# Four places of a one-core hybrid decoder layer re-ordered: a broadcast behind the first scores, two accumulating transfers ahead of a split, one weight copy behind a sum's copy, and the last eighteen row groups summed row by row

## The chip, the cores and the metric

The kernel runs on one core of one Trainium2 chip. The metric is the device time of one execution in microseconds (us). The kernel before was run three times for this; the median is 1169.59 us (1168.78 to 1170.29). One more execution was profiled, and every start, duration and wait below is from that one.

The engines are named as the profile names them: PE is TensorE's matrix multiplication, PEld its weight load, DVE is VectorE, ACT is ScalarE, POOL is GpSimd and SP is SyncE. A letter q behind an engine's name means its instruction queue, such as where it issues a DMA. L1112 is line 1112 of the kernel before.

## The reference, cut to what matters

One layer over 1024 positions of width 1024, all in float32:

```python
h = rmsnorm(x, mix_norm)
q, k, v, su, sv, g_a, g_b = jnp.split(h @ w_in, splits, axis=-1)
y_att = sliding_window_attention(q, k, v, q_norm, k_norm, sinks)     # 8 heads, 2 kv heads, window 128
y_sgu = chunked_spatial_gating(su, sv, sgu_norm, w_s, b_s)
merged = sigmoid(g_a) * (y_att @ w_oa) + sigmoid(g_b) * (y_sgu @ w_ob)
x = x + merged @ w_out
z = rmsnorm(x, ffn_norm) @ w_up                                      # 1024 -> 2 * 2816
zc = conv_b + sum(conv_w[tap] * shifted(z, tap) for tap in range(3)) # causal, by channel
gate, val = jnp.split(zc, 2, axis=-1)
x = x + (silu(gate) * val) @ w_down                                  # 2816 -> 1024
```

## The kernel before

**Precision.** Every float32 operand is kept as two float32r tiles, a high part (an ACT copy, helper `copy_hi`, L88) and a low part (operand minus high part, mostly a subtraction on POOL or DVE). A product is three matmuls: high by high, high by low, low by high.

**Fast products.** The large dense products are cut into 2 by 2 blocks and done with seven block products in place of eight (Strassen's scheme in Winograd's form). The blocks of the left operand are called A11, A12, A22 and the sums S1 to S4, those of the right one B11, B21, B22 and T1 to T4. One block product of the MLP's first half is twelve matmuls of 128x512 (`Blocks.prod`, L1112): four slices of the contraction by three.

**Stages, in order of time.** Key and value projection with the queries (`q_proj`); sixteen attention steps with pieces of other projections between them as filler work for PE; the spatial gating; eight gate pairs; the two branch products; the output projection; the MLP's first half as 22 pairs (`first_pair` for pair 0, `fast_pair` for pairs 1 to 21), one pair being 256 columns of w_up, one gate chunk and one value chunk; and last the product with w_down, in 42 groups of two or one contraction chunks (`mms(g)`, seven block products of six groups each).

**What sets the order.** The order within each engine is that of the Python code, since all stages run under a manual schedule. Each engine takes its instructions one after another; one that waits holds up all behind it on that engine. PE, DVE, ACT, POOL and SP wait for each other by semaphores.

**Around the first place.** `rms_rows` (L135) spreads a column of reciprocal norms over 128 partitions: four small matmuls into a PSUM tile `rb`, then an ACT copy into `rstd_b`. It is called twice at the end of the projection stage, once for each half of the positions; behind it comes attention step 0, which begins with the score matmuls `sc` (`s_mm(0)`) and goes on with a query projection `pq`. The second `rb` takes over the PSUM slot of a transposed query tile that DVE is still splitting (`qs`, L345).

**Around the second place.** Per pair, the left operands come as `lp` (A11, A12) and `lq` (its two halves become S1 and A22) and `s3`. They are loaded by SP; two DMAs that POOL issues (`adds`, L1029 and L1030) then add further blocks of w_up onto `s3` and onto the first half of `lq`. POOL computes S2 and S4 (`sums_r`, into `lr`) and the low parts: `pl` of `lp`, `ql` of `lq` (`split_q`), `s3l`, and the low part of `lr` into the tile `AX` (`split_r`). In `first_pair`, POOL makes the sums of pair 1, then `ql` of pair 1, and then issues the adds for pair 2.

**Around the third place.** At the end of each pair, PE makes the product S2 into `v1`; DVE adds to it, ACT copies the sum into `u2` (L1124), DVE makes two differences and scales (L1130), ACT applies the convolution's last tap (`tap_v`, L1733) and after it copies the next pair's first product into `x1` (L1878). The next pair's A12 is accumulated onto the PSUM tile that this last copy reads. In the code before, the ACT copy of the weight split into `AX` (`split_r` of the next pair) stands ahead of the copy into `u2`.

**Around the last place.** The last block product, M3, adds into four PSUM row blocks X[0] to X[3], two to a PSUM tile (`pdx`). Each group goes through the four row blocks in turn; after the last group, DVE adds the residual into `res` for row blocks 0, 1, 2 (`plus`, L2064), each followed by its store, and then for row block 3 in two halves (L2087), the first stored by ACT and the second by SP.

Of the kernel before, what the change touches and what calls it, by code (L numbers as in the profile page):

```python
# [11 lines left out]
R = mybir.dt.float32r  # L12
# [28 lines left out]
def body(ctx, tc, nc, a):  # L41
# [37 lines left out]
    def PH(s):  # L79
        if psum.get("H") is None:  # L80
            return PS(s)[:, 0:512]
        return psum["H"].tile([128, 512], F, tag="H", name=nm(s))
# [379 lines left out]
    k_lo(1)  # L462
    rms_rows([PH("rb")], rstd, (1,))
    v_split()
# [225 lines left out]
    for n in range(20):  # L690
        if n < 16:
            s_mm(n)
            s_mask(n)
        if 0 <= n - 1 < 16:
            s_exp(n - 1)
# [307 lines left out]
    class Left:  # L1003
# [75 lines left out]
        def split_q(self):  # L1079
            self.split(("S1", "A22"), self.q, *(wst.tile([128, 8, 128], R, tag="w" + x, name=nm("q" + x))  # L1080
                                                for x in "hl"))

        def split_s3(self):
# [712 lines left out]
    def first_pair():  # L1796
# [44 lines left out]
        nx.split_s3()  # L1841
        nx.sums_r()
        nx.split_q()
        lefts[2].adds()
        lefts[2].load_p()
        nc.scalar.copy(u2, q.v1)
# [13 lines left out]
    def fast_pair(n, prev, q, hooks, rms=None):  # L1860
# [56 lines left out]
        if nx:  # L1917
            nx.split_q()
            nx.split_r(n + 1)
            if n + 3 < NPAIR:  # L1920
                lefts[n + 3].load_ahead()
        else:
            hooks[0]()
        q.prod(q.v1, "S2", "T2")
        q.sums(x1, x7, q.v0)
        if not nx:
            hooks[1]()
# [9 lines left out]
    def mlp():  # L1937
# [93 lines left out]
        def mms(g):  # L2031
# [8 lines left out]
            for k in range(k0, k1):  # L2040
                for d in range(4):
                    m = slice(128 * d, 128 * d + 128)
                    for j, (p, q) in enumerate(((ah, bh), (ah, bl), (al, bh))):
                        nc.tensor.matmul(o[d], p[:, k - k0, m], q[:, k - k0, :],  # L2044
                                         start=new and k == 0 and j == 0, stop=k == HK - 1 and j == 2,
                                         skip_group_check=True)

        rs = {}

# [18 lines left out]
        def done(s):  # L2068
            for d in range(4):
# [10 lines left out]
                if s == "M5":  # L2080
                    plus("C22", d, X[d], True)
                if s == "M3" and d < 3:
                    plus("C12", d, X[d], True)
                if s == "M3" and d == 3:
                    t = rs["C12"][:, d, :]
                    for q, c in ((nc.scalar, slice(0, 256)), (nc.sync, slice(256, 512))):
                        nc.vector.scalar_tensor_tensor(t[:, c], X[d][:, c], 0.5, t[:, c], op0=ALU.mult, op1=ALU.add)  # L2087
                        q.dma_start(a["out"][d, :, 512 + c.start:512 + c.stop], t[:, c])
            if s == "M1":
# [30 lines left out]
        for g in range(len(groups)):  # L2120
            mms(g)
            s, k0, k1 = groups[g]
# [25 lines left out]
            if g == 0:  # L2148
                q.tanh()

    with tc.manual_schedule():
# [80 lines left out]
```

## Time and profile before

| what | us |
|---|---|
| median of the three runs | 1169.59 |
| the profiled execution | 1169.8 |
| its span, from the first to the last instruction of the trace | 1168.0 |
| PE busy in the span | 1156.0 |
| POOL busy in the span | 661.0 |
| DVE busy in the span | 853.7 |
| ACT busy in the span | 589.7 |

The profiled execution's time has 1.8 us around the span. Rows of the timeline give the start and the duration of an instruction, its engine, line, operation, output and inputs, and in brackets how long the engine was idle before it and who ended that. Rows of the chain of waits give start, duration, engine, tile and line of the pieces that led to the end, each released by the one above it. A window row gives, for a stretch, each engine's busy time with the number of instructions, then the mean granted clock of TensorE (1.00 is full), the busy share of the DMA engines and their GB/s.

### The profile page before, as it was taken

What the parts mean: (1) busy time and instruction counts of PE and PEld (TensorE: products, weight loads), DVE (VectorE), ACT (ScalarE), POOL (GpSimd) and SP (SyncE); (2) the same over time, 40 slices, a digit from 0 to 9 for tenths busy, and PEclk for the clock granted to TensorE, in tenths of its full rate; (3) what the DMA queues carried; (4) which work ended last, traced back from release to release, by engine and by line L of the source; (5) the groups of instructions that cost most, each with busy time, mean ns of one, the idle gap of its engine ahead of it and who ended that gap; (6) DMA issues with size and microseconds to landing.
All of it is one profiled execution on the core that took longest, in us unless ns stands there. A gap on an engine that the chain in (4) does not pass through costs nothing.

```text
span 1168.0 us, 15816 instructions
## 1 busy us (share of the span) xinstructions
PE 1156.0 (99%) x5784; PEld 981.8 (84%) x5784; DVE 853.7 (73%) x985; ACT 589.7 (50%) x895; POOL 661.0 (57%) x461
## 2 busy tenths in 40 slices
PE   9999999999999999999899999999999999999998
PEld 9899999988888888888788888888888888888886
DVE  7777746734537889877778878887879787866674
ACT  6665568643436546686444444444444454425231
POOL 1668675598783854798776767767677640000000
PEclk9999999999999999999899999999999999999999
DMA  9442575256646766644554545554454368966561
GB/s 367 144 145 56 134 219 189 91 187 192 199 108 236 244 206 234 190 144 132 139 171 126 171 113 159 140 158 127 144 160 138 98 217 299 357 217 200 171 224 55
DMA packets 86429, 204.37 MB, mean 175 GB/s; under 512 B 9616, under 2 KB 17296, under 8 KB 86160
## 3 DMA queue, kind: packets, MB, share of 16 engines
q1 hardware_dynamic: 77280, 174.93, 43.3%
q0 software_dynamic: 8544, 19.93, 10.4%
q10 hardware_dynamic: 528, 8.52, 2.2%
q8 instruction: 45, 0.74, 0.3%
q14 instruction: 32, 0.26, 0.1%
HBM read 162.70 MB, written 57.41 MB: 188 GB/s over the span
## 4 chain that ended last, share of the span: by engine, by line
PE 90%; DVE 3%; POOL 3%; ACT 1%; DMA 1%; issue 1%; SPq 0%; DVEq 0%; POOLq 0%; ACTq 0%
PE pz L1112 51%; PE pdx L2044 10%; PE pd L2044 8%; PE pY L1692 2%; PE pX L1692 2%; PE pvs L94 1%; PE pvs L93 1%; PE pvs L92 1%; PE pu L94 1%; PE pu L92 1%; PE pu L93 1%; PE pv L560 1%; PE pq L92 1%; PE pq L94 1%; PE pq L93 1%
## 5 line engine op out<-in xcount | busy, mean ns | idle before, releaser
L1112 PE MATMUL pz<-T,qh 128*128 128x512 f32 x464 | 143.3, 390 | 0.0
L1112 PE MATMUL pz<-B,ph 128*128 128x512 f32 x352 | 110.5, 396 | 3.3 <-ACT x L1878 3.3
L1112 PEld LDWEIGHTS pz<-T,qh 128*128 128x128 f32 x464 | 87.3, 188 | 18.5 <-ACT u L936 0.3
L1071 POOL TENSOR_TENSOR pl<-lp,ph 128x1024 fp32r<-128x1024 f32 x30 | 72.6, 2421 | 42.5 <-ACT ph L88 42.5
L1112 PE MATMUL pz<-T,ql 128*128 128x512 f32 x232 | 90.3, 389 | 0.0
L1112 PEld LDWEIGHTS pz<-B,ph 128*128 128x128 f32 x352 | 66.9, 191 | 17.6 <-ACT x L1878 3.7
L1130 DVE TENSOR_TENSOR pz<-pz,rstd_b 128x1024 f32<-128x1024 f32 x60 | 74.0, 1233 | 6.1 <-ACT rstd_b L143 4.1
L1071 POOL TENSOR_TENSOR ql<-lq,qh 128x1024 fp32r<-128x1024 f32 (+1 forms) x30 | 75.7, 2522 | 0.1
L1112 PE MATMUL pz<-T,s3h 128*128 128x512 f32 x232 | 71.4, 389 | 0.0
L1112 PE MATMUL pz<-y,wjh 128*128 128x512 f32 x224 | 69.5, 391 | 0.3 <-POOL y L1286 0.3
L1112 PE MATMUL pz<-B,pl 128*128 128x512 f32 x176 | 69.5, 395 | 0.0
L2044 PE MATMUL pdx<-bh,ah 128*128 128x512 f32 x176 | 68.6, 390 | 0.1
L2044 PE MATMUL pdx<-bl,ah 128*128 128x512 f32 x176 | 68.5, 389 | 0.0
L2044 PE MATMUL pdx<-bh,al 128*128 128x512 f32 x176 | 68.5, 389 | 0.0
L88 ACT ACTIVATE qh<-lq 128x1024 fp32r<-128x1024 f32 (+1 forms) x30 | 31.4, 1047 | 69.6 <-POOL pl L1071 28.1
L1071 POOL TENSOR_TENSOR s3l<-lq,s3h 128x512 fp32r<-128x512 f32 x20 | 26.0, 1299 | 70.3 <-ACT s3h L88 70.3
L1352 POOL TENSOR_TENSOR wjl<-wj,wjh 128x512 fp32r<-128x512 f32 (+1 forms) x32 | 42.0, 1334 | 33.6 <-ACT wjh L88 26.9
L1112 PE MATMUL pz<-T,AX 128*128 128x512 f32 x252 | 60.5, 389 | 0.0
L1112 PE MATMUL pz<-B,AX 128*128 128x512 f32 x252 | 60.5, 389 | 0.0
L1738 DVE SCALAR_TENSOR_TENSOR tv<-pz,cp,tv 128x1023 f32<-128x1023 f32 (+1 forms) x44 | 56.2, 1278 | 0.8
L1738 DVE SCALAR_TENSOR_TENSOR tg<-pz,cp,tg 128x1023 f32<-128x1023 f32 (+1 forms) x44 | 56.2, 1278 | 0.8
L1112 PEld LDWEIGHTS pz<-B,AX 128*128 128x128 f32 x252 | 47.3, 188 | 9.8
(386 smaller groups left out, 3562.8 us busy)
## 6 DMA issues: line engine op xcount, KB each, us to landing
lp<-wup SPq DMA_DIRECT2D x22, 512.0 KB, 3.8
lq<-wup SPq DMA_DIRECT2D x22, 512.0 KB, 4.2
ra<-wdown SPq DMA_DIRECT2D x44, 256.0 KB, 4.5
b<-T SPq DMA_DIRECT2D x44, 256.0 KB, 3.8
lq<-wup POOLq DMA_DIRECT2D x42, 256.0 KB, 5.4
B<-tv SPq DMA_DIRECT2D x33, 256.0 KB, 2.3
T<-tt SPq DMA_DIRECT2D x33, 256.0 KB, 2.1
b<-B SPq DMA_DIRECT2D x33, 256.0 KB, 3.1
```

Of the source, the lines that this page charges most:

```text
L88: return nc.scalar.activation(dst, src, AF.Copy, scale=scale)
L92: nc.tensor.matmul(out, wh, mh, start=first, stop=False, **kw)
L93: nc.tensor.matmul(out, wh, ml, start=False, stop=False, **kw)
L94: nc.tensor.matmul(out, wl, mh, start=False, stop=last, **kw)
L560: nc.tensor.matmul(o, vhl[:, kb, g, :], w[:, 2 * g:2 * g + 2, :], start=i == 0 and g == 0, stop=i == len(ops) - 1, skip_group_check=True)
L1071: nc.gpsimd.tensor_tensor(l, r, h.bitcast(F), op=ALU.subtract)
L1112: nc.tensor.matmul(o, p[:, k, :], m, start=not more and k == 0 and j == 0, stop=k == nk - 1 and j == 2, skip_group_check=True)
L1130: nc.vector.tensor_tensor(z, z, rstd_b, op=ALU.mult)
L1352: nc.gpsimd.tensor_tensor(l[:, k], r[:, k], h[:, k].bitcast(F), op=ALU.subtract)
L1692: nc.tensor.matmul(ob[o][e][:, d, :], p[:, 4 * d + k, :], m[:, q, k, :], start=s in (0, 5) and k == 0 and i == 0, stop=k == 3 and i == 2, ...
L1738: nc.vector.scalar_tensor_tensor(t[:, j:], p[:, 0:1024 - j], cw[:, ci, 2 - j:3 - j], t[:, j:], op0=ALU.mult, op1=ALU.add)
L2044: nc.tensor.matmul(o[d], p[:, k - k0, m], q[:, k - k0, :], start=new and k == 0 and j == 0, stop=k == HK - 1 and j == 2, skip_group_check= ...
```

## The change

It has four parts.

1. The second `rms_rows` moves from the end of the projection stage to behind the score matmuls and the mask of attention step 0.
2. In `first_pair`, the adds for pair 2 are issued right behind the sums of pair 1, ahead of the low part `ql` of pair 1; that split is done in two halves, the one for S1 first (`split_q_half`).
3. In `fast_pair`, `split_r(n + 1)` moves from behind `split_q` to behind `q.sums`, so for pairs 1 to 20 the ACT copy into `AX` stands behind the copy into `u2`.
4. The last two groups of M3 are no longer done group by group. `mms_last` takes the row blocks in the order 2, 0, 1, 3, for each all nine matmuls of the three contraction chunks. The residual add of row block 2 is written behind its matmuls, those of 0 and 1 behind row block 1's, and the two halves of row block 3 at the end.

```diff
@@ -460,7 +460,6 @@
     rms_rows([PH("rb")], rstd, (0,))
     k_lo(1)
-    rms_rows([PH("rb")], rstd, (1,))
     v_split()
@@ -691,6 +690,8 @@
             s_mm(n)
             s_mask(n)
+        if n == 0:
+            rms_rows([PH("rb")], rstd, (1,))
         if 0 <= n - 1 < 16:
@@ -1080,6 +1081,13 @@
+        def split_q_half(self, i):
+
+            if i == 0:
+                self.qt = [wst.tile([128, 8, 128], R, tag="w" + x, name=nm("q" + x)) for x in "hl"]
+            k = slice(4 * i, 4 * i + 4)
+            self.split((("S1", "A22")[i],), self.q[:, k], *(t[:, k] for t in self.qt))
+
@@ -1839,9 +1847,11 @@
         nx.split_s3()
-        nx.sums_r()
-        nx.split_q()
+        nx.sum_s2()
+        nx.sum_s4()
         lefts[2].adds()
+        nx.split_q_half(0)
+        nx.split_q_half(1)
         lefts[2].load_p()
@@ -1916,13 +1926,14 @@
             nx.split_q()
-            nx.split_r(n + 1)
             if n + 3 < NPAIR:
                 lefts[n + 3].load_ahead()
         else:
             hooks[0]()
         q.prod(q.v1, "S2", "T2")
         q.sums(x1, x7, q.v0)
+        if nx:
+            nx.split_r(n + 1)
@@ -2045,6 +2056,23 @@
+        def mms_last():
+
+            two = [(k, k - groups[g][1], ops_[g]) for g in (len(groups) - 2, len(groups) - 1)
+                   for k in range(*groups[g][1:])]
+            for d in (2, 0, 1, 3):
+                m = slice(128 * d, 128 * d + 128)
+                for k, i, (ah, al, bh, bl) in two:
+                    for j, (p, q) in enumerate(((ah, bh), (ah, bl), (al, bh))):
+                        nc.tensor.matmul(X[d], p[:, i, m], q[:, i, :], start=False,
+                                         stop=k == HK - 1 and j == 2, skip_group_check=True)
+                for x in {2: (2,), 1: (0, 1)}.get(d, ()):
+                    plus("C12", x, X[x], True)
+            t = rs["C12"][:, 3, :]
+            for q, c in ((nc.scalar, slice(0, 256)), (nc.sync, slice(256, 512))):
+                nc.vector.scalar_tensor_tensor(t[:, c], X[3][:, c], 0.5, t[:, c], op0=ALU.mult, op1=ALU.add)
+                q.dma_start(a["out"][3, :, 512 + c.start:512 + c.stop], t[:, c])
```

The old lines of `done` for M3 go, `mms(g)` is called for all but the last two groups, and `mms_last()` is called behind the loop.

On PE, at the end of the projection stage, the order before (`rb` is the broadcast, `sc` the scores of attention step 0, `pq` a query projection):

```order
L383 MATMUL pk_603<-ident,kr 128x128 x4
L140 MATMUL rb_622<-ident,rstd 128x128 x4
L140 MATMUL rb_630<-ident,rstd 128x128 x4
L485 MATMUL sc_657<-kT_107,qs_589 128x256 x2
L488 MATMUL sc_657<-kT_107,qs_589 128x256 x2
L485 MATMUL sc_657<-kT_107,qs_589 128x256 x2
L488 MATMUL sc_657<-kT_107,qs_589 128x256 x2
L92 MATMUL pq_674<-wq_102,x_4_117 128x256
```

And the same place of the change:

```order
L383 MATMUL pk_603<-ident,kr 128x128 x4
L140 MATMUL rb_622<-ident,rstd 128x128 x4
L484 MATMUL sc_651<-kT_107,qs_589 128x256 x2
L487 MATMUL sc_651<-kT_107,qs_589 128x256 x2
L484 MATMUL sc_651<-kT_107,qs_589 128x256 x2
L487 MATMUL sc_651<-kT_107,qs_589 128x256 x2
L140 MATMUL rb_666<-ident,rstd 128x128 x4
L92 MATMUL pq_674<-wq_102,x_4_117 128x256
```

The second broadcast has moved behind the eight score matmuls and now stands right ahead of the query projection.

On POOL, in `first_pair`, the order before (`lr` holds pair 1's sums S2 and S4, `ql` and `AX` are low parts for pair 1, the two DMA rows are the adds for pair 2, `s3l` is pair 2's):

```order
L664 TENSOR_TENSOR lr_5593<-lq_5468,lp_5466 128x512
L664 TENSOR_TENSOR lr_5593<-lp_5466,lr_5593 128x512
L1071 TENSOR_TENSOR ql_5597<-lq_5468,qh_5596 128x1024
L1029 DMA lq<-wup 128x512
L1030 DMA lq<-wup 128x512
L1071 TENSOR_TENSOR AX_5636<-lr_5593,AX_5636 128x1024
L1071 TENSOR_TENSOR s3l_5679<-lq,s3h_5678 128x512
```

And the same place of the change:

```order
L663 TENSOR_TENSOR lr_5593<-lq_5468,lp_5466 128x512
L663 TENSOR_TENSOR lr_5593<-lp_5466,lr_5593 128x512
L1030 DMA lq<-wup 128x512
L1031 DMA lq<-wup 128x512
L1072 TENSOR_TENSOR ql_5599<-lq_5468,qh_5598 128x512 x2
L1072 TENSOR_TENSOR AX_5638<-lr_5593,AX_5638 128x1024
L1072 TENSOR_TENSOR s3l_5681<-lq,s3h_5680 128x512
```

The two DMAs stand ahead of `ql`, which is two instructions now; the rest is as it was.

On ACT, from the end of pair 1 into pair 2, the order before (`AX` is the high part of pair 2's sums, `u` the copy into `u2`, `tv` the tap, `x` the copies into `x1` and `x7`):

```order
L1758 ACTIVATE pz_5441<-tg_5659 128x1024
L88 ACTIVATE qh_5725<-lq 128x1024
L88 ACTIVATE AX_5636<-lr_5708 128x1024
L1124 COPY u_716_5644<-pz_5443 128x512
L1733 ACTIVATE tv_5766<-pz_5443,cp 128x1024
L1878 COPY x_731_5768<-pz_5762 128x512
```

And the same place of the change:

```order
L1766 ACTIVATE pz_5441<-tg_5661 128x1024
L88 ACTIVATE qh_5727<-lq 128x1024
L1132 COPY u_716_5646<-pz_5443 128x512
L88 ACTIVATE AX_5638<-lr_5710 128x1024
L1741 ACTIVATE tv_5768<-pz_5443,cp 128x1024
L1888 COPY x_731_5770<-pz_5764 128x512
```

The copies of the weight and of the sum have changed places, here and in the same way in every pair up to the twentieth.

11 lines of the change are left out of this document (3 added, 8 removed).

## The prediction, made before the changed kernel was run

> **What bounds the kernel now.** I read the page first, for the engines' busy time; then the list of who waited for whom, for PE; then windows around PE's longest wait, for the granted clock; then the chain of waits into that wait.
>
> ```profile
> PE 1156.0 (99%) x5784; PEld 981.8 (84%) x5784; DVE 853.7 (73%) x985; ACT 589.7 (50%) x895; POOL 661.0 (57%) x461
> PE pz L1112 <- ACT x L1878: 3.3, 1, 3.3
> PE rb L140 <- DVE qs L345: 1.1, 1, 1.1
> 953.39 29.92 PE pdx L2044 x132
> PEclk9999999999999999999899999999999999999999
> ```
>
> PE is busy for 1156.0 of 1168.0 us, and the change neither adds nor removes a matmul. So there are only three things to win: time in which PE waits, time in which it runs slowly, and the ends of the span. Two waits are over 1 us, 3.3 us at L1112 and 1.1 us at L140; the change touches what ends both. The fourth row gives PE's pace: 29.92 / 132 = 0.2267 us from one 128x512 matmul to the next. The fifth is the granted clock in 40 slices of the span, in tenths: it falls in one slice alone, the one with the longer wait.
>
> The windows around the longer wait:
>
> ```profile
> 571.45:574.88 3.43, 0.15 (x1) 0.00 (x0) 3.36 (x4) 1.68 (x2) 2.04 (x1) 0.89 0.59 202
> 574.88:580.17 5.29, 5.29 (x13) 4.13 (x13) 5.04 (x5) 2.29 (x4) 2.99 (x3) 0.50 0.08 7
> 580.17:581.00 0.83, 0.83 (x4) 0.66 (x2) 0.00 (x0) 0.83 (x1) 0.00 (x0) 0.53 0.98 173
> ```
>
> The wait costs twice. PE could have started its next matmul at 571.45 and starts it at 574.88: 3.43 us. Then the granted clock is 0.50 until 581.00. The twelve matmuls of pair 2's A12 take 5.29 us where 12 x 0.2267 = 2.72 would do (2.57 lost), the next two 0.83 us in place of 0.45 (0.38 lost). Together 3.43 + 2.95 = 6.38 us hang on this one wait.
>
> The chain into it:
>
> ```profile
> 551.48 2.34 POOL ql L1071
> 553.82 5.79 DMA lq<-wup
> ...
> 565.86 1.25 POOL lr L664
> ...
> 567.19 1.64 POOL lr L664
> ...
> 568.85 1.06 ACT AX L88
> 569.92 0.48 ACT u L1124
> ...
> 573.15 1.20 ACT tv L1733
> ```
>
> POOL issues pair 2's adds only after `ql`; the transfer lands at 559.6; ACT waits for it with `s3h`, and everything behind on ACT and POOL is late; the sums end at 568.83, ACT copies them into `AX`, and only then takes the copy into `u2` on which the tail up to `x1` hangs. From the start of the `u2` copy to PE's start the tail is 574.88 - 569.9 = 5.0 us.
>
> **Part 2 and 3, the stall in pair 2.** What the two parts must bring: PE is free at 571.45, so the `u2` copy must start by 571.45 - 5.0 = 566.4, 3.5 us earlier.
>
> ```profile
> 555.02 3.06 POOL L1071 TENSOR_TENSOR AX<-lr,AX 128x1024 fp32r<-128x1024 f32 x1
> 555.12 0.62 PE L1112 MATMUL pz<-T,qh 128*128 128x512 f32 x2
> 556.47 2.59 DVE L1738 SCALAR_TENSOR_TENSOR tg<-pz,cp,tg 128x1023 f32<-128x1023 f32 x2
> 561.18 1.01 ACT L1758 ACTIVATE pz<-tg 128x1024 f32<-128x1024 f32 x1
> 564.74 2.93 DVE L664 TENSOR_TENSOR tt<-tv 128x512 f32<-128x512 f32 x1
> 567.59 0.68 DVE L1123 TENSOR_TENSOR pz<-x1f,pz 128x512 f32<-128x512 f32 x1
> DMA to landing us min/median/max: 3.9/4.0/5.8
> ```
>
> The adds are now issued at 551.48, 2.34 us earlier. They hold POOL for 555.02 - 553.82 = 1.20 us, so the S1 half of `ql` runs from 552.7 and is done at 553.9 (a POOL subtraction of that size takes 1.25 in the chain above), the other half at 555.2. PE's product S1 starts at 555.12, so the half split hides the two DMAs that are now ahead of it; without it `ql` would be whole only at 555.0, on the edge. `AX` starts 0.2 us later than before and ends near 558.3; PE reads it 24 matmuls (5.4 us) after 555.12, so at 560.6.
>
> The first add lands between 551.48 + 3.9 = 555.4 and, if it comes no earlier at all, 559.6 (the last row is L1029's over all pairs). I take the trip this very transfer had, 5.79, so 557.3, since the same SP loads are beside it. Then `s3h` is done at 557.9, and what sets ACT's tanh (L1758) is no longer the transfer but DVE's convolution, which ends at 556.47 + 2.59 = 559.06. So tanh starts 561.18 - 559.06 = 2.12 us earlier. From tanh to DVE's add into `v1` (L1123) it was 567.59 - 561.18 = 6.41 us of gating and a subtraction of 2.93 us; unshortened, the add starts at 565.5 and ends at 566.15. With part 3 the `u2` copy follows at once, at 566.2, ahead of the limit of 566.4. So the stall goes, with 0.2 us to spare on the unshortened count. That subtraction is of the size of L1123's 0.68 us, so up to 2.2 us more may be in hand; a residue of a few tenths is as possible. The sums, some 2 us earlier too, end near 566.8; the copy into `AX` then lies in the 3.3 us between `u2` and `tv` in which ACT only waits for DVE. **Value: -6.4 us**; from 0 (the wait stays) to -6.4, which is all there is.
>
> A rule weighed: the Trainium skill, TensorE: Matmul & The Clock Gate, Part 1, has half clock after an idle window of about 3.4 us and full clock again after about 3.4 busy ones. The fall behind 3.43 us agrees; the slow stretch here is 6.1 us. By the page's length it would cost about half of 3.4, an estimate of 1.7 in place of 2.95, and the time after the change would be 1.2 us more; the measured 2.95 decides.
>
> **Part 3 in the other pairs.** Moving `AX` behind `u2` adds a wait to 19 more pairs: POOL's low part of `AX` now waits for a copy that waits for the sum, and `s3l`, the adds and `pl` queue behind it on POOL.
>
> ```profile
> 722.36 1.06 ACT L88 ACTIVATE AX<-lr 128x1024 fp32r<-128x1024 f32 x1 [1.97 <-POOL lr L664]
> 723.33 0.57 ACT L1124 COPY u<-pz 128x512 f32<-128x512 f32 x1
> 724.66 2.40 POOL L1071 TENSOR_TENSOR AX<-lr,AX 128x1024 fp32r<-128x1024 f32 x1
> 730.92 1.30 POOL L1071 TENSOR_TENSOR s3l<-lq,s3h 128x512 fp32r<-128x512 f32 x1 [3.87 <-ACT s3h L88]
> ```
>
> In this pair the sum is there at 722.93 (L1123 ends), the `AX` copy would end near 724.6, and POOL wants it at 724.66: nothing lost. If it came 1 us late, POOL's 3.87 us of idleness ahead of `s3l` takes it. PE never waits in these pairs, so the 0.4 us by which `u2` comes earlier brings nothing. Value 0; to be felt, the delay must pass 3.9 us.
>
> **Part 1, the broadcast.**
>
> ```profile
> 40.89 1.29 DVE L407 TENSOR_TENSOR vt<-pkv,rstd 128x512 f32<-128x512 f32 x2 [0.80 <-POOL rstd L447]
> 42.21 0.86 DVE L345 TENSOR_TENSOR qs<-pqt,qs 64x256 fp32r<-64x256 f32 x2
> 43.22 1.13 PE L140 MATMUL rb<-ident,rstd 128*128 128x128 f32 x8 [1.15 <-DVE qs L345]
> 44.10 0.48 PE L485 MATMUL sc<-kT,qs 128*128 128x256 f32 x2
> 45.12 0.28 PE L92 MATMUL pq<-wq,x 128*128 128x256 f32 x1
> ```
>
> The second `rb` waits for DVE's `qs`, done at 43.07. The scores take 45.12 - 44.10 = 1.02 us; they need an older `qs` and the PSUM slot that the first of the two L407 instructions frees near 41.5, so they fit into PE's idle 1.15 us. Then `rb` starts at 43.22 as before and `pq` at 44.10. ACT's copy of `rb` moves behind other short copies, and its reader is a multiplication after a whole filler projection. **Value: -1.0 us** (bounds 0, if a later wait for another engine swallows it, and -1.15). I take the full amount because PE's other waits behind it are 0.3 us and the chain into them starts at PE, so they move with it.
>
> **Part 4, the end.**
>
> ```profile
> 1163.29 0.69 DVE res L2064
> 1163.90 0.74 DVE L2087 SCALAR_TENSOR_TENSOR res<-pdx,res 128x256 f32<-128x256 f32 x2
> out<-res SPq DMA_DIRECT2D x1, 128.0 KB, 2.2
> ```
>
> Row block 2 shares a PSUM tile with row block 3, so its add starts with PE's last matmul at 1163.29, and the halves of row block 3 queue behind it at 1163.90. In the change, row block 2 is 27 matmuls (6.1 us) and blocks 0 and 1 are 9 (2.0 us) ahead of the end, and their adds of 0.69 each are over; the halves start at 1163.29, 0.61 us earlier. The last transfer lands 2.2 us after issue, behind three of 256 KB; now one of those is long gone and the others issued earlier. **Value: -0.7 us**, from -0.6 (the adds alone) to -1.3 (another 0.69 for the transfer out of the way). The last group's operands are needed 18 matmuls (4.1 us) earlier; DVE has had nothing to do for over 10 us by then.
>
> **Sum.** 1169.8 (span 1168.0 and 1.8 around it) - 6.4 - 1.0 - 0.7 = 1161.7 us for the profiled execution; it lies 0.2 above the median of the runs, so 1161.5 us.
>
> **Rivals.**
>
> A. The adds land no earlier, because the DMA engines are full anyway.
>
> ```profile
> q0 software_dynamic: 490, 0.91, 27.4%
> q1 hardware_dynamic: 432, 1.31, 17.6%
> ```
>
> These rows are for 545 to 566: of 21 us the adds' queue takes 5.8 and SP's loads 3.7, and all of the loads and half of the adds lie between 552.5 and 559.6, which they nearly fill. If the loads go first, `s3h` stays where the transfer lands, at 559.6, and only the changed order helps: `u2` at 568.3 (L1123 ends at 568.27) in place of 569.9, PE at 573.3, a wait of 1.9 us. The clock then holds or falls; the trace has one fall, after 3.43 us, and 1.9 is well below. If it holds, 1.6 + 2.95 + 1.7 are won: 1163.4 us. If it falls, 1166.3. Against A: the add is asked for first. The Trainium skill, DMA: Bandwidth & Descriptors, Queues, rings and completion order, has each DMA engine going round between its queues, which would let the first add land well before both are through; no run here shows that yet.
>
> B. The wait of pair 2 stays because something else is as late, and only parts 1 and 4 count: 1169.6 - 1.7 = 1167.9 us. For it: the margin on my count is 0.2 us. Against it: two of the chain's links are taken out, and either alone shortens it.
>
> C. Slower. Issuing the adds just as SP issues its loads holds POOL past 1.20 us. It decides from 2.9 us on: then the S1 half of `ql` is later than 555.58, where PE reads it. If POOL is held for the trip, 5.79, the half is ready at 558.5, PE waits 2.9 us, and a clock fall adds 2.95. Behind that the old wait shrinks to 1.5 us by the changed order, 1.9 less than before, with its own fall: +5.9 - 1.9 - 1.7 = +2.3, so 1171.9 us. Against it: POOL went on 1.20 us after the first issue while the same loads were in flight.
>
> **How the numbers follow.** Forecast 0.72; A with the clock held 0.13, with a fall 0.05; B 0.07; C 0.03. The range goes from 1160.4 (part 4 at its -1.3, and half a microsecond for the spread of the runs) to 1164.4 (A with the clock held, without part 1's gain); it leaves out A's fall, B and C, 0.15. About 0.2% (2.3 us) is what a measurement can tell from no change. Faster by more: 0.72 + 0.13 + 0.05 = 0.90; within it: B, 0.07; slower: 0.03.
>
> **What would show it.** Right: no wait of PE at L1112 near 570 and a granted clock of 1.00 there; `s3h` of pair 2 by 558; tanh right behind the convolution; scores ahead of `rb` with PE's wait there near 0.4 us; the last two adds right at PE's end. Wrong: `s3h` still near 559 (A), a wait of PE above 3 us and clock 0.50 (B), a wait of PE near 555 (C), or new waits in pairs 3 to 21, which would say that part 3 was not free.

## The result, and the profile after

The changed kernel takes 1162.45 us, the median of four runs (1162.16 to 1163.07); the kernel before took 1169.73 us beside it (1168.78 to 1170.29). The ratio is 0.9939, with a 95% interval from 0.9922 to 0.9957. That is 7.3 us less, where 8.1 were predicted, and inside the predicted range. The profiled execution took 1162.16 us, 2.0 of them around its span.

The page of the changed kernel, its engines' busy time and the granted clock in 40 slices:

```profile
PE 1152.5 (99%) x5784; PEld 978.5 (84%) x5784; DVE 853.1 (74%) x985; ACT 589.9 (51%) x896; POOL 662.5 (57%) x462
PEclk9999999999999999999999999999999999999999
```

The list of who waited for whom, two rows for PE (us in total, times, longest):

```profile
PE pz L1120 <- ACT x L1888: 0.4, 1, 0.4
PE rb L140 <- DVE qs L345: 0.2, 1, 0.2
```

The windows around the place where the stall was (the stretch, its length, busy time of PE, PEld, DVE, ACT and POOL, granted clock, DMA share, GB/s):

```profile
569.89:570.48 0.59, 0.16 (x1) 0.00 (x1) 0.59 (x1) 0.54 (x2) 0.59 (x1) 1.00 0.70 278
570.48:573.34 2.86, 2.86 (x13) 2.36 (x13) 2.83 (x4) 2.20 (x3) 1.06 (x2) 1.00 0.26 105
```

The wait for ACT's copy `x` at A12 of pair 2 went from 3.3 us to 0.4, the one at `rb` from 1.1 to 0.2, and the clock no longer falls: A12 takes 2.86 us in place of 5.29.

Where the time went, stretch by stretch, from the starts of the same matmuls in both profiles. Counted from 0 along PE, matmul 344 is the first `pq` of attention step 0, 3064 the first of sixteen small ones right ahead of A11 of pair 1 (the expectations below call it the start of A11), 3204 the first of A12 of pair 2, 3400 one in pair 4:

| stretch of the span, us | before | after | gained | predicted |
|---|---|---|---|---|
| up to matmul 344 | 45.12 | 44.14 | 0.98 | 1.0 |
| 344 to 3064 | 498.18 | 497.61 | 0.57 | 0 |
| 3064 to 3400 (the stall) | 79.00 | 73.62 | 5.38 | 6.4 |
| 3400 to PE's end | 540.95 | 540.94 | 0.01 | 0 |
| PE's end to the span's end | 4.77 | 3.82 | 0.95 | 0.7 |

The chain of waits of the changed kernel through the stall (start, duration, engine, tile, line; each released by the one above):

```profile
549.91 6.77 DMA lq<-wup
...
556.77 0.63 ACT s3h L88
...
558.26 1.01 ACT pz L1766
...
559.29 1.25 DVE pz L1769
...
560.56 1.24 DVE tv L1770
...
561.82 2.94 DVE tt L663
...
564.76 0.62 DVE pz L1131
...
565.40 0.60 ACT u L1132
...
568.75 1.21 ACT tv L1741
569.96 0.48 ACT x L1888
```

POOL's `ql` and `lr` and the copy into `AX`, which stood in the chain before, are out of it. But the transfer still stands at its head, and its trip (from issue to landing) has grown from 5.79 to 6.77 us.

The timeline of the two places in which the small parts work, and of PE at the start of A12 (start, duration, engine, line, operation, tiles; in brackets the idle time before and who ended it):

```profile
42.66 0.40 PE L487 MATMUL sc<-kT,qs 128*128 128x256 f32 x2
43.25 1.13 PE L140 MATMUL rb<-ident,rstd 128*128 128x128 f32 x8 [0.20 <-DVE qs L345]
44.14 0.37 PE L92 MATMUL pq<-wq,x 128*128 128x256 f32 x1
...
570.48 0.73 PE L1120 MATMUL pz<-B,ph 128*128 128x512 f32 x2 [0.43 <-ACT x L1888]
...
1155.92 0.39 PE L2067 MATMUL pdx<-bh,al 128*128 128x512 f32 x1
1156.35 0.76 DVE L2073 SCALAR_TENSOR_TENSOR res<-pdx,res 128x256 f32<-128x256 f32 x2 [0.75 <-PE pdx L2067]
1157.13 0.33 SPq L2074 DMA_DIRECT2D out<-res  x1
```

And the DMA view of the last store by SP (its size and the us from issue to landing):

```profile
out<-res SPq DMA_DIRECT2D x1, 128.0 KB, 1.8
```

The scores now stand in the gap ahead of `rb`, and the two last additions stand right at PE's end.

### The profile page after: what moved, and what is told of

It is laid out like the page before. It is cut to its first block, busy times and chain, and to the rows that moved or that the text cites. A ratio compares the mean times of both kernels' runs of the same rounds, so it can differ in the third digit from the quotient of the medians.

```text
span 1160.1 us, 15819 instructions
## 1 busy us (share of the span) xinstructions
PE 1152.5 (99%) x5784; PEld 978.5 (84%) x5784; DVE 853.1 (74%) x985; ACT 589.9 (51%) x896; POOL 662.5 (57%) x462
## 4 chain that ended last, share of the span: by engine, by line
PE 85%; DVE 5%; POOL 3%; DMA 2%; ACT 2%; issue 1%; SPq 0%; DVEq 0%; ACTq 0%; POOLq 0%
PE pz L1120 51%; PE pdx L2055 10%; PE pd L2055 8%; PE pY L1700 2%; PE pX L1700 1%; PE pu L94 1%; PE pu L92 1%; PE pu L93 1%; PE pv L559 1%; DMA xr<-xw 1%; PE pq L92 1%; PE pq L94 1%; PE pq L93 1%; POOL sq L1547 1%; DMA xt<-xt 1%
## 5 line engine op out<-in xcount | busy, mean ns | idle before, releaser
L2055 PE MATMUL pdx<-bh,ah 128*128 128x512 f32 x164 | 63.9, 390 | 0.1
L2055 PE MATMUL pdx<-bl,ah 128*128 128x512 f32 x164 | 63.8, 389 | 0.0
L2055 PE MATMUL pdx<-bh,al 128*128 128x512 f32 x164 | 63.8, 389 | 0.0
L1120 PEld LDWEIGHTS pz<-T,AX 128*128 128x128 f32 x252 | 47.3, 188 | 9.8
```

Source lines behind the costliest of these rows:

```text
L1120: nc.tensor.matmul(o, p[:, k, :], m, start=not more and k == 0 and j == 0, stop=k == nk - 1 and j == 2, skip_group_check=True)
L2055: nc.tensor.matmul(o[d], p[:, k - k0, m], q[:, k - k0, :], start=new and k == 0 and j == 0, stop=k == HK - 1 and j == 2, skip_group_check= ...
```

## The experiments

Each experiment is the changed kernel with one edit, unless it says otherwise. The theory at the outset: parts 2 and 3 remove the stall by shortening one chain (transfer, tanh, sums, `u2`, `x1`), and parts 1 and 4 bring their microsecond each where they stand. The rivals: the transfer sets the end whatever the order; something in DVE's queue does; the rest is chance. The first four take out one part each; the kernel before ran at 1168.4 us (1166.52 to 1171.16) on that chip. By their times the kernels without part 1, 2 or 4 (ratios 0.9963, 0.996 and 0.9959) cannot be told from the changed kernel's second measurement further down (0.9958); only the one without part 3 (0.9985) stands apart. What parts 1, 2 and 4 are worth is read from their stretches of the profiles.

### Part 1 taken out

```diff
     k_lo(1)
+    rms_rows([PH("rb")], rstd, (1,))
     v_split()
...
-        if n == 0:
-            rms_rows([PH("rb")], rstd, (1,))
```

> The changed kernel with the broadcast put back ahead of the first scores (part 1 undone). Theory, part 1 is worth the scores' 1.0 us: PE waits 1.15 us again at the second broadcast and the kernel takes 1163.4 us, against 1162.45 of the change. Rival 1, a later wait takes the gain back: 1162.5 us and the same start of the MLP as in the change. Rival 2: in the change the 256-column matmuls of the gating projection near 175 us went on at 0.1133 us each and before at 0.1178, which alone is 1.2 us; if part 1 is what sets their pace, undoing it costs 2 us or more (1164.6).

Measured: 1164.42 us (1162.97 to 1165.9), ratio 0.9963 (0.995 to 0.9975). The wait at `rb` is 1.1 us again and matmul 344 starts at 45.31. Part 1's own place does not account for the rest: the wait at A12 of pair 2 is 1.2 us, and 3064 to 3400 takes 74.42 us. A second profile of this kernel, further down, comes back to that. Rival 2 is out, though the time is near its 1164.6: matmuls 1250 to 1560, with the projection at 175 us among them, take 35.24 us here, as in the changed kernel's first profile, so the fast pace does not need part 1.

### Part 4 taken out

```diff
         for g in range(len(groups)):
-            if g < len(groups) - 2:
-                mms(g)
+            mms(g)
...
-        mms_last()
```

The residual additions of M3 are back in `done`.

> The changed kernel with the last two groups done group by group, as before (part 4 undone). Theory, the adds of the last row block queue behind that of row block 2 for 0.6 us and the last transfer lands 0.4 us later behind more traffic: 1.0 us more, 1163.4 us, with 1.4 us from PE's end to the last issue in place of 0.8. Rival, the transfers alone set the end and the order of the adds nothing: less than 0.4 us more.

Measured: 1164.13 us (1162.87 to 1164.52), ratio 0.9959 (0.9945 to 0.9974). From PE's end (1157.73) to the span's end it is 4.76 us, where the kernel before had 4.77 and the changed one 3.82. The timeline of its end:

```profile
1156.41 2.05 DVE L2092 SCALAR_TENSOR_TENSOR res<-pdx,res 128x512 f32<-128x512 f32 x3 [10.69 <-PE pdx L2055]
...
1158.38 0.75 DVE L2115 SCALAR_TENSOR_TENSOR res<-pdx,res 128x256 f32<-128x256 f32 x2
```

Three full additions run up to 1158.4, 0.7 us past PE's end, before the halves may start. So part 4 is worth 0.95 us, and alone makes them; from PE's end to the last issue it is 1.42 us, where 1.4 was expected.

### Part 2 taken out: the adds behind the split again

```diff
-        lefts[2].adds()
         nx.split_q_half(0)
         nx.split_q_half(1)
+        lefts[2].adds()
```

> The changed kernel with the two accumulating transfers issued behind the split again (part 2 undone, part 3 kept). Theory: the first add lands near 558, tanh of pair 1 starts 1.5 to 2 us later than in the change, and PE waits 1.9 to 2.4 us for the copy into x1 near 570, in place of 0.4. Then either the clock holds, since the only fall seen came behind 3.4 us: 1164.1 us; or it falls behind a wait of this length too: 1167.0 us. Rival, the place of the adds does not matter and part 3 alone removes the wait: 1162.5 us.

Measured: 1163.84 us (1163.32 to 1164.82), ratio 0.996 (0.9945 to 0.9975). The wait is 1.2 us, the clock stays at 1.00, and 3064 to 3400 takes 74.45 us: part 2 is worth 0.8 us beside part 3. The wait expected was 1.9 to 2.4 us. ACT's `s3h` starts 15.87 us behind matmul 3064 (559.46), against 15.02 in the changed kernel: though the adds are issued 2.5 us later, they land only 0.85 us later. One profile could show a chance here, but all of them together say the same: `s3h` starts 15.45 to 16.39 us behind matmul 3064 in the four profiles with the adds behind the split (15.90 on average), and 14.91 to 15.84 in the nine that have the adds ahead of it and no other edit to that copy (15.13): 0.8 us.

### Part 3 taken out: the copy into AX ahead of u2 again

```diff
             nx.split_q()
+            nx.split_r(n + 1)
...
         q.sums(x1, x7, q.v0)
-        if nx:
-            nx.split_r(n + 1)
```

> The changed kernel with the weight copy into AX ahead of the sum's copy again in all pairs (part 3 undone, part 2 kept). Theory: in pair 1 the copy into u2 starts when AX is written, near 567.0 in place of 565.4, so PE waits 1.6 us longer, 2.0 us in all; clock holding, 1164.0 us, clock falling, 1166.9 us. Rival, with the adds early the AX copy is out of the way: 1162.5 us. If part 3 costs the other pairs something, this kernel is faster than the theory says by that amount.

Measured: 1166.47 us (1165.35 to 1169.51), ratio 0.9985 (0.9975 to 0.9996). PE's timeline at A12:

```profile
573.55 1.22 PE L1120 MATMUL pz<-B,ph 128*128 128x512 f32 x2 [2.00 <-ACT x L1888]
```

And the windows from the gap on:

```profile
571.40:573.55 2.15, 0.15 (x1) 0.00 (x0) 2.12 (x3) 1.68 (x2) 0.81 (x1) 0.99 0.55 211
573.55:577.00 3.45, 3.45 (x8) 2.80 (x9) 3.41 (x4) 2.20 (x3) 1.52 (x2) 0.51 0.00 0
577.00:578.00 1.00, 1.00 (x6) 0.79 (x6) 0.96 (x2) 0.00 (x0) 1.00 (x2) 1.00 0.00 0
```

The wait is 2.0 us, and behind it the clock falls: A12 takes 4.41 us, 1.7 more than its 12 x 0.2267. The stretch takes 76.42 us: part 3 is worth 2.8. In the chain of this kernel ACT's copy into `AX` waits for POOL's sum up to 567.5, and `u2` waits behind it, though the transfer lands as early as in the changed kernel (`s3h` 15.11 us behind matmul 3064). From matmul 3400 to 5000 it takes 362.67 us, as in the kernel before (362.67) and in the changed one (362.67): in the other pairs part 3 does nothing.

### The changed kernel again, beside the next three

The kernel before ran at 1168.88 us (1167.8 to 1169.9) on this chip.

> The changed kernel once more, beside the others on this chip. Two readings of the profiles so far differ. (a) What differs between profiles ahead of 545 us (the pace of the 128x256 matmuls between 172 and 202 us, 0.113 us apart in one profile and 0.118 in four others, and a 0.5 us wait on POOL cl or on ACT pm) varies from execution to execution: then the span here may lie 1 to 2 us above the first profile's 1160.1 us, the wait for ACT x ahead of A12 of pair 2 lies between 0.4 and 1.2 us with the trip of the two adds (6.8 us gave 0.4, 7.6 gave 1.2), and the time is 0.993 to 0.996 of the kernel before. (b) The first profile shows the change's own effect: pace 0.113, span 1160 within 0.5 us, the wait 0.4, ratio 0.9935 to 0.9945.

Measured: 1163.78 us (1163.01 to 1164.94), ratio 0.9958 (0.9943 to 0.9973), span 1162.9. Reading (a) holds: the stretch of the stall takes 73.62 us as in the first profile, with the same wait of 0.4, while all that differs lies ahead of it. Grouped by line and shape, the 128x256 matmuls between 172 and 202 us, in the changed kernel's first profile (count, then busy time and mean ns):

```profile
L94 PE MATMUL pvs<-wvB,x 128*128 128x256 f32 x55 | 15.2, 276 | 0.0
```

And in this one:

```profile
L92 PE MATMUL pvs<-wvB,x 128*128 128x256 f32 x54 | 15.2, 281 | 0.0
```

It is the same code, 2% apart. From matmul 1250 to 1560 that makes 35.24 or 36.48 us. And here PE waits 1.4 us for a DVE tile (`ac`) that no other profile shows. The 0.57 us gained between matmuls 344 and 3064 are chance of this kind: over all profiles that stretch takes 498.8 us on average in the nine with part 1 and 498.4 in the five without, and single ones lie up to 2.6 us apart.

### Stores and their subtraction behind the sums, pair 1 alone

```diff
-        prev.stores()
+        if not rms:
+            prev.stores()
...
         q.sums(x1, x7, q.v0)
...
+        if rms:
+            prev.stores()
```

> Pair 1 alone issues the stores of the gated product and its contended DVE subtraction (2.94 us) behind the sums of the next products, not ahead of them. Theory: that subtraction stands on the path to the x1 copy, so the wait ahead of A12 of pair 2 (0.43 us in the first profile of the changed kernel) goes to 0, and the copy comes 0.4 to 2.9 us earlier; the time falls 0.4 to 0.8 us against the changed kernel, PE clock at 1.00. Rival: DVE is not what sets it (the transfer of the adds and the split copies on ACT are, and what stands behind them is cut elsewhere): the wait stays at 0.3 us or more and the time is the same within 0.2 us. Second rival: the subtraction, moved, meets the scaling of the next sums and delays the convolution: a new wait of 0.3 us or more between 571 and 592 us.

Measured: 1163.27 us (1162.96 to 1164.57), ratio 0.9955 (0.994 to 0.997). A12 of pair 2 follows S3 without a gap, and up to matmul 3400 it takes 73.30 us in place of 73.62. DVE and ACT in its timeline:

```profile
563.84 0.59 ACT L1132 COPY u<-pz 128x512 f32<-128x512 f32 x1 [2.53 <-DVE pz L1131]
...
567.06 2.48 DVE L663 TENSOR_TENSOR tt<-tv 128x512 f32<-128x512 f32 x1
...
568.71 0.57 ACT L1888 COPY x<-pz 128x512 f32<-128x512 f32 x1
```

So the subtraction did stand on the path: with it out of the way, `u2` starts 4.52 us behind the tanh (559.32) where it was 7.14. Part of the gain is given back later: matmuls 3240 to 3400 take 36.99 us in place of 36.59, since the moved subtraction still takes 2.48 us of DVE, now ahead of pair 1's last scaling: the convolution ends 2.64 us behind the start of PE's S1 of pair 2, where it was 2.24. So the wait went, as the theory has it, and the second rival came true as well: pair 3's A12, at 590.7 us, now waits 0.59 us in place of 0.19.

### The tanh ahead of the transfer's copy, pair 1 alone

```diff
-        if nx:
+        if nx and not rms:
             nx.split_s3()
-        if n + 2 < NPAIR:
+        if n + 2 < NPAIR and not rms:
             lefts[n + 2].adds()
...
         prev.tanh()
+        if rms:
+            nx.split_s3()
+            lefts[n + 2].adds()
```

> Pair 1 alone issues the split of S3 and the two adds of pair 3 behind the split copy of p and the tanh, not ahead of them, so on ACT the tanh no longer stands behind the copy that waits for the adds' transfer. Theory: the wait that is left (0.43 us ahead of A12 of pair 2) comes from that transfer by ACT's order alone: tanh then begins at the end of the convolution (557.5 instead of 558.26 in the first profile's time, 0.7 to 0.8 earlier, and more where the trip of the adds is longer), the wait goes to 0 and the time falls 0.4 us (up to 1.2 where the trip is long). Rival: the copy of p, or the convolution, holds the tanh just as long: it moves less than 0.3 us and the wait stays above 0.2. Second rival: the adds of pair 3, 1.5 to 2 us later, land too late for pair 3: a new wait of PE near 590 us of over 0.5 us.

Measured: 1163.13 us (1162.94 to 1165.5), ratio 0.9958 (0.9941 to 0.9975). On ACT:

```profile
555.75 1.06 ACT L88 ACTIVATE ph<-lp 128x1024 fp32r<-128x1024 f32 x1
559.10 1.03 ACT L1766 ACTIVATE pz<-tg 128x1024 f32<-128x1024 f32 x1 [2.28 <-DVE tg L1746]
560.06 0.61 ACT L88 ACTIVATE s3h<-lq 128x512 fp32r<-128x512 f32 x1
```

The bracket names DVE's convolution now, not the DMA. The wait at A12 is gone, and the stretch takes 73.03 us; 3240 to 3400 takes 36.57 of them, as in the changed kernel, so the later adds cost pair 3 nothing. So in the changed kernel the tanh was held by ACT's order alone, behind a copy that waits for the transfer and that it has no need of.

### The split of q in one piece

```diff
-        nx.split_q_half(0)
-        nx.split_q_half(1)
+        nx.split_q()
```

> The split of q in the first pair is one operation of 1024 elements again, still behind the adds. Theory: the halves themselves are worth little, since the whole of ql would be ready about 0.1 us after or before PE first reads it at 554.0 us: a wait of 0 to 0.2 us there, the time the same within 0.3 us. Rival: the halves carry part 2: a wait of PE on POOL ql of 1 us or more near 554 us, and the time 1 us or more above the changed kernel.

Measured: 1162.2 us (1161.39 to 1163.49), ratio 0.9945 (0.993 to 0.9959). PE's timeline where it first reads `ql`, and at A12:

```profile
553.88 0.61 PE L1120 MATMUL pz<-T,qh 128*128 128x512 f32 x2
554.55 0.50 PE L1120 MATMUL pz<-T,ql 128*128 128x512 f32 x1
...
570.33 0.39 PE L1120 MATMUL pz<-T,s3l 128*128 128x512 f32 x1
570.79 0.74 PE L1120 MATMUL pz<-B,ph 128*128 128x512 f32 x2
```

`ql` is read 0.67 us behind the row ahead of it, where it is 0.45 in the changed kernel: a wait of 0.2 us. Then A12 waits that much less, 0.46 us from start to start in place of 0.82, and the stretch takes 73.67 us in place of 73.62. The halves are worth nothing, as long as a wait stands behind them.

### The kernel before with one edit: the tap behind the x1 copy

```diff
             prev.last_sum()
-            prev.tap_v()
             x1, x7, q.u2 = temp("x1"), temp("x7"), temp("u2")
...
         nc.scalar.copy(x1, q.g0)
+        if not rms:
+            prev.tap_v()
```

None of the four parts is in it. The kernel before ran at 1168.26 us (1167.34 to 1170.04) here, and beside the next three.

> The kernel before, with one edit alone: from pair 2 on, ACT takes the first tap of the pair ahead behind the x1 copy, not ahead of it; none of the change's four parts. Theory: A12 waits for x1, x1 needs nothing but A11 (its last matmul starts at 568.5 us in the kernel before), and it stands behind the tap only by ACT's order; so the stall is a queue on ACT and not a want of data. Then x1 follows the u2 copy (569.82 to 570.39), ends near 570.9, A12 of pair 2 starts within 0.3 us of PE's pace (571.45) instead of at 574.88, the clock stays at 1.00, and the later taps cost 0 to 0.5 us at the next pair: 5.5 to 6.4 us less than the kernel before, ratio 0.9945 to 0.9955. Rival: the chain of DVE is the limit whatever ACT's order: it comes back as waits of PE on the x7 copy (576.64 in the kernel before) or at pair 3 that together take 3 us or more, and less than 3.5 us is gained.

Measured: 1167.86 us (1166.38 to 1168.89), ratio 0.9993 (0.9984 to 1.0003). The stall does go: `x1` follows `u2` at once, A12 starts on time, the clock stays full, and 3064 to 3400 takes 74.05 us. And the gain is given back:

```profile
570.06 0.56 ACT L1124 COPY u<-pz 128x512 f32<-128x512 f32 x1
570.52 0.59 ACT L1877 COPY x<-pz 128x512 f32<-128x512 f32 x1
...
583.79 0.68 DVE L664 TENSOR_TENSOR x<-x,pz 128x512 f32<-128x512 f32 x1
584.52 3.01 PE L1112 MATMUL pz<-B,AX 128*128 128x512 f32 x12 [0.85 <-DVE x L664]
957.27 0.50 PE L2045 MATMUL pdx<-bh,al 128*128 128x512 f32 x1 [0.58 <-DVE al L2016]
```

The first two rows are ACT, the third DVE, the last two PE. PE is on time, but DVE is nearly as late as in the kernel before: the last scaling of pair 1's sums ends 30.7 us behind matmul 3064, in the two profiles of the kernel before 31.7 and 31.2, in the changed kernel 28.8. The product S4 may not add onto its PSUM half before DVE has subtracted that half from `x7` (583.79), and PE waits there. Counted from matmul 3064 on, PE has won 6.4 us on the first profile of the kernel before when A12 and the slow stretch of that profile are over. It loses 1.1 of them at 584.5, 1.4 in pieces of 0.1 to 0.3 up to 950 us, 1.0 at 957 and 0.7 at 988. From matmul 3064 to PE's end it takes 617.81 us in place of 619.95. Against the second profile of the kernel before, further down, it wins 4.6 us and keeps 0.8. Neither expectation held as written: ACT's order did make the stall, and DVE's lateness, no matter to A12, comes back as other waits. The rival's number was the better one (less than 3.5 us gained), but its waits lie further on than it said. Parts 2 and 3 are worth their time because they bring DVE's chain forward, and not only the copy.

### The changed kernel with the same edit

The diff is the one above, in the changed kernel.

> The changed kernel with the same one edit: from pair 2 on the first tap of the pair ahead stands behind the x1 copy on ACT. Theory: the 0.43 us wait ahead of A12 of pair 2 and the 0.2 us one near 590 us go, whatever the adds' trip takes: from the start of A11 of pair 1 to the 3400th matmul (73.62 us in the changed kernel) it takes 73.0 us, with no new wait, and the time falls 0.6 us, too little for the measured ratio to show by itself. Rival: the taps, later, delay the convolutions, and a later pair waits: that stretch is 73.6 us or more, or the 3400th to the 5000th matmul take over 362.7 us.

Measured: 1162.1 us (1161.41 to 1162.94), ratio 0.9943 (0.9926 to 0.9959). PE's timeline at the same place:

```profile
571.48 0.39 PE L1120 MATMUL pz<-T,s3l 128*128 128x512 f32 x1
571.71 0.61 PE L1120 MATMUL pz<-B,ph 128*128 128x512 f32 x2
```

0.23 us from one to the next, which is PE's pace: no wait. 3064 to 3400 takes 72.57 us, and 3400 to 5000 the usual 362.67. So the wait near 590 us went too, which is more than the 73.0 expected. This is the best of the kernels by its profile, 1.05 us less than the changed kernel in that stretch; by the runs it cannot be told from it.

### The kernel before, a second profile

> The kernel before, a second profile. If the 0.5 us wait on POOL cl between 45 and 172 us belongs to the change (it stands in four of eight profiles that have the earlier scores, and in the one that hasn't), this profile has none, as the first, and the 1250th matmul starts within 0.3 us of 172.06. If it falls by chance, it may stand here too, and that matmul starts up to 1 us away. In either case the rest, from A11 of pair 1 to the 3400th matmul, takes 79.0 us within 0.1, with a wait of 3.3 us and the clock at 0.50 behind it.

Measured: 1168.1 us (one run), span 1166.35. There is no wait on POOL's `cl`, and matmul 1250 starts at 172.23, but the stretch of the stall is not the 79.0 us expected: it takes 77.16.

```profile
574.05 1.22 PE L1112 MATMUL pz<-B,ph 128*128 128x512 f32 x2 [2.81 <-ACT x L1878]
571.08:574.05 2.97, 0.16 (x2) 0.01 (x1) 2.94 (x3) 1.68 (x2) 1.60 (x1) 0.96 0.57 193
574.05:577.40 3.35, 3.35 (x8) 2.67 (x9) 3.31 (x4) 2.20 (x3) 1.42 (x2) 0.53 0.00 0
577.40:578.40 1.00, 1.00 (x6) 0.79 (x6) 0.96 (x2) 0.00 (x0) 1.00 (x2) 1.00 0.00 0
```

The wait is 2.8 us in place of 3.3, and the slow stretch of the clock 3.35 us in place of 6.1. So the stall differs by nearly 2 us between these two executions, and with it what there is to win: 5.4 us against the first profile, 3.5 against this one. What this profile saves in the stall it does not keep whole: at the place near 957 us where the swap alone lost 1.0 us, it loses 0.5 (3400 to PE's end takes 541.49 us, where the changed kernel and every variant of it take 540.9).

### Part 1 taken out, a second profile

> The changed kernel without part 1, a second profile. In its first profile the adds' trip took 7.6 us and the wait ahead of A12 of pair 2 was 1.2 us, while five profiles with part 1 had 0.4. If that falls by chance, the trip is about 6.8 us here and A11 of pair 1 to the 3400th matmul take 73.6 us as in the changed kernel; if it comes from the missing part 1, they take 74.4 us again. The wait at rb is 1.1 us in either case, as in the kernel before.

Measured: 1164.45 us (one run), span 1162.4. The wait at `rb` is 1.1 us; the one at A12 is 0.6 and not 1.2, the adds' trip 6.99 us and not 7.6, and the stretch 73.79 us. So most of the longer wait of this kernel's first profile was the transfer's chance. Whether the rest was too is not settled: of the nine profiles with the adds ahead of the split, these two without part 1 have the latest `s3h` (15.84 and 15.23 us behind matmul 3064; the others 14.91 to 15.11).

## Why the prediction was right, and what it mis-sized

**Part 1, -1.0 us: right.** Its own stretch gained 0.98. Over all profiles, matmul 344 starts at 44.37 us on average in the nine with the part (44.03 to 44.74) and at 45.27 in the five without (45.12 to 45.47): 0.9 us. No later wait swallows it in a regular way: at matmul 1250 the averages are 171.87 and 172.67, 0.8 apart. At matmul 3064 they are still 0.5 apart, beside a spread of 2.8 us, so the times of the runs cannot show this part. What comes and goes there, 0.5 us waits on `cl` or `pm`, stands in kernels with and without the part.

**Parts 2 and 3, -6.4 us: the mechanism right, the size 1.0 us too large.** All there was to win was indeed that much in the profile that the prediction went by: with the swap added, where PE has no wait left, the stretch takes 79.00 - 72.57 = 6.43 us less; of the second profile's 77.16 it would be 4.6. The step that failed is the trip of the adds, "I take the trip this very transfer had, 5.79, so 557.3". It was 6.77 us. The adds were issued 2.36 us earlier (8.16 us behind matmul 3064, before 10.52), and `s3h` started only 1.37 earlier (15.02 behind it, before 16.39); the rest went to the longer trip. The reason given for 5.79, "since the same SP loads are beside it", is where this went wrong: before, SP had issued its three loads (551.5 to 552.4 us) 1.4 to 2.3 us ahead of the first add, and now issues them 0.1 to 0.9 us behind it (550.0 to 550.85). The sign "`s3h` of pair 2 by 558" holds in absolute time (556.77) only because all of it comes 1.55 us earlier; counted from matmul 3064 the copy is 0.3 us late. So what sets the tanh is not the convolution, as predicted, which ends at 554.91 + 2.59 = 557.50, but still the transfer through ACT's order, at 558.26. The 0.76 us between them eat the "0.2 us to spare". The steps behind held to the hundredth: from tanh to `u2` 7.14 us, predicted 559.06 to 566.2; the subtraction was not shortened, 2.94 us. What is left is a gap of 0.59 us at A12, 0.14 in a slower A12, and 0.3 near 590 us, where pair 3's `x1` copy is late by as much, now that PE comes earlier: 1.05 together. Taken out singly, part 2 costs 0.8 us and part 3 2.8; that is what both win against the second profile of the kernel before (77.16 - 73.62 = 3.54). The first profile's 5.38 has 0.5 us more of a wait and 1.3 more of slow clock.

**Rival A** was thus half true: of the earlier issue, two fifths were lost to the transfer in this pair of profiles, and two thirds by the averages over all of them (0.8 us won of 2.4). Its sign would have been a wait of 1.9 us; that wait comes with part 3 taken out instead, where the transfer is as early as ever and the copy into `AX` holds `u2`. The Trainium skill, DMA: Bandwidth & Descriptors, Queues, rings and completion order, has each DMA engine go round between its queues; a trip that grows from 5.79 to 6.77 us when all of SP's loads are issued behind it agrees with sharing, though no run here separates the queues.

**The clock.** Its stretch of 2.95 us was right for the profile it came from, and is not a constant. With part 3 out, and in the second profile of the kernel before, the fall cost 1.7 and 1.6 us (A12 takes 4.41 and 4.32 us in place of 2.72). That is what was estimated from the Trainium skill, TensorE: Matmul & The Clock Gate, Part 1, which has full clock again after about 3.4 busy us: 3.45 and 3.35 us here, and 6.1 in the first profile alone. Finer windows of the kernel before show where its fall lies:

```profile
571.60:574.10 2.50, 0.00 (x1) 0.00 (x0) 2.43 (x4) 0.95 (x1) 1.89 (x1) 1.00 0.73 246
574.20:574.88 0.68, 0.00 (x0) 0.00 (x0) 0.68 (x1) 0.63 (x2) 0.00 (x0) 0.50 0.00 0
574.88:580.96 6.08, 6.08 (x14) 4.79 (x15) 5.04 (x5) 3.08 (x4) 2.99 (x3) 0.50 0.20 28
580.96:581.10 0.14, 0.14 (x2) 0.10 (x1) 0.00 (x0) 0.14 (x2) 0.00 (x0) 1.00 1.19 219
```

The clock fell while PE still waited. The trace's own record has it at 0.50 from 574.13 to 580.96, which is 6.83 us, or twice the 3.41 of the other two falls (573.50 to 576.92 with part 3 out, 573.80 to 577.21 in the second profile). The stretches of full clock between changes are whole multiples of 3.413 us as well, in all fourteen profiles. So, as far as these traces go, the clock changes on a grid of 3.41 us that lies elsewhere in each execution. In the slot of the grid that ended with the fall, PE had idled for 2.53, 1.95 and 2.56 us (first profile, part 3 out, second profile); slots with 1.24 us (part 1 out, part 2 out) and 1.41 (the wait for `ac`) brought no fall. The first profile's next slot held another 0.75 us of the wait and stayed slow too; in the other two that rest was 0.05 and 0.25 us, and the clock came back. That the fall cost 2.95 us and not 1.7 was thus the chance of where the grid lay.

**Part 3 in the other pairs, 0: right.** 362.67 us from matmul 3400 to 5000 with it and without; the 0.5 us more in the second profile of the kernel before is the wait near 957 us.

**Part 4, -0.7 us: right in place, 0.25 small.** The tail went from 4.77 to 3.82 us, and back to 4.76 without the part. The last issue now follows PE's end by 0.82 us (1157.13 - 1156.31), 0.6 sooner than before, as predicted; the last transfer takes 1.8 us in place of 2.2, which was allowed for only in the range.

With the measured sizes the sum is 1169.8 - 5.4 - 0.9 - 0.95 - 0.2 = 1162.35 us; 1162.45 was measured. That it meets to 0.1 us is luck in part, since the stall's 5.4 is that of one profile. In the second comparison the changed kernel lay at 0.9958 of the kernel before, 5.1 us less and not 7.3. A smaller stall, as in the second profile of the kernel before, would give about that (3.5 + 0.9 + 0.95 = 5.35); but the pace of the 128x256 matmuls and the wait for `ac` differ by as much between executions, and no run here separates them. So the change is worth 5 to 7 us; in differences the prediction's range is 5.2 to 9.2 us less, which holds the first comparison and just misses the second.

## What to carry to other kernels

When a stall is charged to a copy, ask for the copy's own inputs: here `x1` needed nothing but a product long done, and stood behind a tap, a transfer and a tanh only by the order of one engine's queue. But a queue that is put right moves the wait to whoever is late in truth: compare the swap alone, which won 5 us in the stretch of the stall and gave over half of that back, with parts 2 and 3, which made the late engine earlier. And when a transfer is issued earlier into a busy stretch, count on a part of the lead only: here 1.4 of 2.4 us in the first pair of profiles, and 0.8 on average.

## What the runs showed of the hardware

- The clock fell behind PE gaps of 2.15, 2.97 and 3.43 us (part 3 out, and two profiles of the kernel before), and held behind 1.41 us (part 1 out) and 0.59. The Trainium skill, TensorE: Matmul & The Clock Gate, Part 1, has the fall after an idle window of about 3.4 us; the 2.15 us are well short of that. How long it stays low, 3.41 or 6.83 us here, is worked out above.
- Matmuls of 128x256 run at 276 or 281 ns, the same throughout a stretch and different between executions of one kernel, at a granted clock of 1.00 in both. Of the fourteen profiles four have the fast pace (35.24 us from matmul 1250 to 1560), two of them without part 1, and ten the slow one (36.42 to 36.48). Why is not known.
- A DVE subtraction of 128x512 takes between 686 and 2936 ns, depending on what POOL does beside it: 686 with nothing of POOL's beside it (at 940.1 us), 973 to 984 beside the end of `pl` and the start of one `lr`, 2936 beside `pl` and two `lr`. The row that groups them in the changed kernel, minimum, median and maximum:

```profile
L663 DVE TENSOR_TENSOR tt<-tv x11: 686/980/2936, 561.8 to 940.1; 128x512 f32<-128x512 f32 x11
```

The longest is the one on the path of the stall. It ends 0.56 us behind the first `lr`. The Trainium skill, SBUF — State Buffer, SBUF: two separate sides, has the later of two instructions wait until the first is through, when one is DVE's with two SBUF inputs and the other POOL's and reads SBUF. The trace agrees in kind, and moving the subtraction took it out of the path, though not out of DVE's time (2.48 us where it went).
